# Hybrid encoder block on one core: queue places of seven small products counted over a whole group, and one gate block moved to the second inversion

## The chip, the core and the metric

One core of a Trainium2 chip runs the whole layer. The metric is device time in microseconds (us) of one execution, taken several times; the profile is of one more execution by the hardware profiler. Five engines work side by side, each through its own queue in order: TensorE (PE, matrix products into PSUM banks; its loads of the stationary operand are PEld), VectorE (DVE), ScalarE (ACT), GpSimd (POOL) and SyncE (SP, which here only starts DMA transfers). They wait for each other by semaphores.

## The reference

The input is 2048 tokens of width 1024, in float32, through one layer:

```
h   = RMSNorm(x);  P = h @ w_in          # q/k/v, RWKV-7 r/k/v + low-rank w/a/g, 2048 gate columns
yA  = chunk-band attention               # own chunk of 64 and 8 before it, 8 heads
yB  = RWKV-7 time mixing                 # 8 heads of 64, state 64 x 64, a scan over time
m   = sigmoid(gA) * (yA @ proj_a) + sigmoid(gB) * (yB @ proj_b)
x   = x + RMSNorm(m @ w_out)
x   = x + RMSNorm(relu(RMSNorm(x) @ w_up)^2 @ w_down)
```

The part around the change is yB. A step of its scan is `state = state * w + (state a) b^T + v k^T; y = state r`, and beside each head's output there is a bonus `sum(r * k * r_k) * v`.

## The kernel before

**Precision.** Each large float32 product is made of three: both operands are split into a high part (a cast on ScalarE, L70) and a low part (a subtraction on VectorE, L71), and high x high, high x low and low x high are added in PSUM (`mm3`, L80).

**Dense blocks.** `dense` gives 128 columns of `h @ w_in` for a group of 512 tokens: it loads 512 KB of weights on SyncE's queue (two buffers), splits them, and issues 8 x 3 = 24 products of 128 x 128 by 128 x 512 into one of two banks.

**Groups and stages.** The tokens go in four groups of 512. For each group come `phase_rwkv` (30 dense blocks: 14 of the recurrent branch, 16 gates), `phase_attention` and `phase_merge`; after all groups the feed-forward part follows, in two halves.

**The recurrent stage.** The 8 heads are four pairs (p = 0 to 3; a pair fills 128 partitions), and the scan is made chunk by chunk of 64 tokens:

- `rwkv_pre` projects r, k, v of a pair (three dense blocks, `mix`), forms decays and scaled operands on VectorE, ScalarE and GpSimd, the bonus (L488, two products: high and low part of r), transposes (L497), and the score products inside each chunk (L517): two halves of four chunks, 16 products each, with two banks a half, which VectorE reads into NA, AR and BR (L526 to L533).
- `rwkv_inverse` inverts the chunk matrices of two pairs. VectorE builds the inverses of 32 x 32 blocks by 31 steps, one after the other (L551, L557), then turns them (X1, L560; XD, L562); ScalarE and GpSimd copy XD to XT (L567, L569).
- `rwkv_blocks` completes 64 x 64 from the 32 x 32 blocks: 64 tiny products (L582, NA by X1), a copy to Z on ScalarE (L585), 64 more (L590, Z by XT), a copy to XT (L594).
- `rwkv_trans` makes each chunk's transition out of that (ps_at L609, ps_w L616, ps_ug L626, ps_tq L637, ps_s L650, ps_y L654), and `recurrence` steps through the 8 chunks (L665 to L668). `rwkv_post` normalises (transposes at L693) and writes out.

The first inversion (pairs 0 and 1) has its elimination beside dense blocks of gates and of pair 2, and its transitions between the work of pairs 2 and 3; the second (pairs 2 and 3) stands beside gates alone, near the group's end.

**Order of dense blocks in a group**, counted from 1: low-rank w/a; r, k, v of pair 0; gates 0, 1; r, k, v of pair 1; gates 2, 3; low-rank g; gate 4; r, k, v of pair 2; r, k, v of pair 3; gates 5 to 9; gate 10; gate 11 in the loop over 19 steps of the second transitions at i = 3, gate 12 at i = 9; gates 13, 14, 15 behind it. Each is 24 products, so product 0 of block n has the number 24 (n - 1) in the group's count.

**What sets the order in the queues.** The code is written with generators that are advanced by turns, and a planner then lists each engine's instructions by its own costs and the order written. Where this order isn't wanted, `queue_behind` adds an edge without a semaphore: this product stands behind that one in TensorE's queue. `blocks_behind` uses it for the first product of L582 and of L590: behind products 3 and 12 of the k block of pair 3 (first inversion), and behind products 11 and 20 of gate 11 (second inversion).

Of the kernel before, what the change touches and what calls it, by code (L numbers as in the profile page):

```python
# [32 lines left out]

GATES = (0, 0, 1, 0, 0, 0, 0, 1)
STEPS = (1, 2, 1, 1, 1, 1, 1, 1, 1, 1, 1, 0, 0, 2, 1)
DEC = math.exp(-0.5)

ATT0 = 0
# [12 lines left out]
class Block:  # L51
# [33 lines left out]
        info = mybir.DependencyInfo(mybir.DependencyClass.NoSync, mybir.DependencyReason.DATA)  # L85
        self.tc.add_manual_dep(ins, first.name, info, reason="order of TensorE's queue")

    def blocks_behind(self, *places):

        for ins, i in zip(self.blocks, places):  # L90
            self.queue_behind(ins, self.mm[i])

    def dense(self, col):

        wh, wl = self.wsplit(
            self.a["w_in"][:, col : col + P].rearrange("(k p) n -> p k n", p=P), "w", KB, P
        )
        ps = self.pd.tile([P, G], F32, tag="d", name="psd")
        self.mm = self.mm3(ps, [(wh[:, k], wl[:, k], self.h[0][:, k], self.h[1][:, k]) for k in range(KB)])
        return ps  # L100

    def rstd(self, pool, ssq, scale, eps, post=None):
# [274 lines left out]
    def rwkv_pre(self, g, p, rp, NA, between=lambda: None):  # L377
# [10 lines left out]
        nc.scalar.activation(tw, ps, AF.Tanh, scale=0.5, bias=self.hw0[:, col])  # L388
        k = self.tmp("k")
        self.mix(g, 4 + p, k)  # L390
        if p == 3:
            self.blocks_behind(3, 12)

        ps = self.lora(1, p)
        ta = self.tmp("ta")
# [89 lines left out]

        psb = self.pa.tile([P, G], F32, tag="a", name="ps_bonus")
        for i, x in enumerate((rh, rl)):
            nc.tensor.matmul(psb, self.bones, x, start=i == 0, stop=i == 1)  # L488
        nc.vector.tensor_tensor(r, psb, v, ALU.mult)
        nc.gpsimd.dma_start(self.bvd[p], r)  # L490

# [17 lines left out]
        for h in range(2):  # L509
            cs = slice(h * 4, h * 4 + 4)  # L510

            both = [self.pa.tile([P, 4, P], F32, tag="a", name="ps_A") for _ in range(2)]
            for j in range(4):
                c = h * 4 + j
                for par, psA in enumerate(both):
                    rw = slice(par * C, par * C + C)
                    nc.tensor.matmul(  # L517
                        psA[:, j].rearrange("p (s t) -> p s t", t=C),
                        BK[rw, c].rearrange("p s t -> p (s t)"),
                        AR[rw, c, par : 3 : 2 - par], start=True, stop=True,  # L520
                    )
            for par, psA in enumerate(both):
                ow = slice(C - par * C, P - par * C)
                for lo, w in ((0, C), (32, 32)):
                    hw = slice(par * C + lo, par * C + lo + 32)
                    nc.vector.tensor_tensor(  # L526
                        NA[hw, q, cs, 0:w],
                        psA[hw, :, lo : lo + w],
                        n2[hw, cs, par, None].to_broadcast((32, 4, w)),
                        ALU.mult,  # L530
                    )
                nc.vector.tensor_tensor(AR[ow, cs, par], psA[ow, :, 0:C], mS[ow], ALU.mult)
                nc.vector.tensor_tensor(BR[:, cs, par, 1], psA[:, :, C:P], mN[:, par, cs], ALU.mult)  # L533
# [35 lines left out]
            nc.gpsimd.tensor_copy(XT[par * C : par * C + 32, :, :, 0:32], XD[par * C : par * C + 32])  # L569
        self.X1, self.XT = X1, XT  # L570

    def rwkv_blocks(self, NA, Rs):

        nc, X1, XT = self.nc, self.X1, self.XT
        first, second = [], []
        Z = self.ip.tile([P, 2, NC, 32], F32, tag="Z", name="Z")
        parts = [(slice(r, r + 32), slice(r + 32, r + C)) for r in (0, C)]
        ps = self.pa.tile([P, 2, NC, 32], F32, tag="a", name="ps_t1")
        for q in range(2):
            for c in range(NC):  # L580
                for lo, hi in parts:
                    mm = nc.tensor.matmul(ps[hi, q, c], NA[lo, q, c, 32:64], X1[lo, q, c], start=True, stop=True)  # L582
                    first.append(mm.ins)
        for lo, hi in parts:
            nc.scalar.copy(Z[hi], ps[hi])  # L585
        ps = self.pa.tile([P, 2, NC, 32], F32, tag="a", name="ps_t2")
        for q in range(2):
            for c in range(NC):
                for lo, hi in parts:
                    mm = nc.tensor.matmul(ps[lo, q, c], Z[hi, q, c], XT[hi, q, c, 32:64], start=True, stop=True)  # L590
                    second.append(mm.ins)
        self.blocks = first[0], second[0]
        for lo, hi in parts:
            nc.scalar.copy(XT[lo, :, :, 32:64], ps[lo])  # L594
        for q in range(2):
            Rs[q]["XT"] = XT[:, q]
# [119 lines left out]
    def phase_rwkv(self, g, quads):  # L716
        tc = self.tc
        with ExitStack() as ctx:
            def pool(name, bufs, **kw):
                return ctx.enter_context(tc.tile_pool(name=name, bufs=bufs, reuse_waits="tile", **kw))  # L720

            rp = pool("rw", 3)
            self.tp = pool("rwt", 9)
            self.ip = pool("rwi", 1)
            self.xp = pool("rwx", 2)
            self.lp = pool("rwl", 1)
            self.sp = pool("rws", 2)
            self.pa = pool("rwpa", 2, space=PSUM)
            self.pr = pool("rwpr", 2, space=PSUM)
            self.py = pool("rwpy", 2, space=PSUM)  # L730

            def pairs():
                return self.ip.tile([P, 2, NC, C], F32, tag="NA", name="NA")

            gates = iter(range(2 * KB))

            def gate(n=1):
                for i in range(n):
                    i = next(gates, None)
                    if i is not None:  # L740
                        self.gate(i)

            def places(plan, act):
                it = iter(plan)
                return lambda: act(next(it, 0))

            def rec_of(NA, Rs, b):
                self.rwkv_blocks(NA, Rs)
                yield
                for q in range(2):  # L750
                    yield from self.rwkv_trans(2 * b + q, Rs[q])
                    yield
                yield from self.recurrence(b, Rs)

            self.lora_wa(g)
            NA = pairs()
            between = places(GATES, gate)
            Rs = [self.rwkv_pre(g, q, rp, NA, between) for q in range(2)]
            if g == 0:
                self.bias_corners()  # L760
            inv = self.rwkv_inverse(NA, rp)
            for _ in range(2):
                advance(inv, 8)
                gate()
            advance(inv, 6)
            self.lora_g(g)
            advance(inv)
            gate()
            rec = rec_of(NA, Rs, 0)
            NA = pairs()  # L770
            between = places(STEPS, lambda n: advance(rec, n))
            nxt = [self.rwkv_pre(g, 2 + q, rp, NA, between) for q in range(2)]
            inv = self.rwkv_inverse(NA, rp)
            for n in (1, 4):
                advance(rec, n)
                gate()
            advance(rec)
            post = [self.rwkv_post(q, Rs[q]) for q in range(2)]
            for p in post:
                advance(p, 1)  # L780
            sums = []

            def load(b):
                sums.append(next(quads)(b))
                advance(sums[-1], 1)

            for i in range(3):
                advance(inv, 8)
                gate()
                if i == 0:  # L790
                    b = rp.tile([P, 4, G], F32, tag="BR", name="cmb")
                    load([b[:, i] for i in range(4)])
                elif i == 1:
                    b, c = (rp.tile([P, n, G], F32, tag=t, name="cmb") for t, n in (("AR", 3), ("SV", 2)))
                    load([b[:, 0], b[:, 1], b[:, 2], c[:, 0]])
            advance(inv)
            for p in post:
                advance(p)
            gate()
            rec = rec_of(NA, nxt, 1)  # L800
            load([self.tmp("cmb") for _ in range(4)])
            ops = chain(*sums)
            for i in range(19):
                advance(rec, 1)
                if i == 1:
                    load([self.tmp("cmb") for _ in range(4)])
                if i > 3:
                    advance(ops, 1)
                if i in (3, 9):
                    gate()  # L810
                if i == 3:
                    self.blocks_behind(11, 20)
            advance(rec)
            gate()
            for _ in range(2):
                advance(sums[-1], 2)
                gate()
            post = [self.rwkv_post(2 + q, nxt[q]) for q in range(2)]
            for p in post:
                advance(p, 1)  # L820
            gate(2 * KB)
            for p in post:
                advance(p)

# [680 lines left out]
```

## Time and profile before

| | |
|---|---|
| median of 3 runs | 3324.03 us (3318.0 to 3327.82) |
| profiled execution | 3325.37 us, its span 3323.7 us |
| mean granted TensorE clock | 0.993 |
| TensorE busy | 3198.8 us, 96% of the span |
| VectorE busy | 2248.2 us, 68% |
| ScalarE busy | 1581.6 us, 48% |
| GpSimd busy | 592.7 us, 18% |
| moved by DMA | 592.56 MB |

The span runs from the first to the last instruction; the rest of the profiled execution's time lies around it. A row of a timeline gives start, duration, engine, line, operation, output<-inputs, shapes and count, and in brackets the engine's idle time just before with what ended it. A matrix product's duration covers its way through the array, and the next starts before it ends; the distance between two starts is the rate of issue. Windows give the busy time of each engine in a stretch, the granted TensorE clock (1.00 is full), the DMA share and GB/s. The recurrent stage of the first group lies between 24 and 307 us of the span, those of the other groups end near 791, 1308 and 1828 us.

### The profile page before, as it was taken

To read this page: it belongs to the slowest core of one execution; us is meant where nothing else is said; L and a number is where in the kernel's file an instruction comes from. 1 tells how busy PE (TensorE), PEld (TensorE's weight loads), DVE (VectorE), ACT (ScalarE), POOL (GpSimd) and SP (SyncE) were. 2 spreads that over 40 slices of the span, in tenths; PEclk is the share of its full clock that TensorE was granted. 3 is DMA by queue.
4 is the path that set the end of the run, shared out by engine and by line. 5 is a ranking of instruction groups with operands and counts; after the bars stand their busy time and mean duration, and the time that the engine had idled before them with its cause. 6 is when DMAs were issued, how large, how long until landed. Compare 5 with 4: busy or idle time off the path is not lost. (4 is left out here: it accounts for less than half of the span.)

```text
span 3323.7 us, 50325 instructions
## 1 busy us (share of the span) xinstructions
PE 3198.8 (96%) x18913; PEld 2597.9 (78%) x18913; DVE 2248.2 (68%) x3719; ACT 1581.6 (48%) x2575; POOL 592.7 (18%) x1093
## 2 busy tenths in 40 slices
PE   7999999999999999999999999999999999999998
PEld 5777778777877777877777787878788878788887
DVE  5775666786766876775876675777656757775565
ACT  3434634434644434654444663545543444454333
POOL 2222002222102222101222100121211112220000
PEclk9999999999999999999999999999999999999999
DMA  5335374247465336655325647664787875547565
GB/s 151 89 118 186 114 232 126 80 137 241 156 215 154 91 104 229 198 170 186 96 77 187 208 121 246 231 199 143 240 285 232 300 250 193 168 161 235 191 214 179
DMA packets 449692, 592.56 MB, mean 178 GB/s; under 512 B 26324, under 2 KB 313248, under 8 KB 449448
## 3 DMA queue, kind: packets, MB, share of 16 engines
q1 hardware_dynamic: 392488, 413.14, 40.1%
q0 software_dynamic: 47744, 159.42, 13.2%
q10 hardware_dynamic: 9216, 16.78, 1.4%
q8 instruction: 149, 2.44, 0.3%
q14 instruction: 95, 0.78, 0.1%
HBM read 425.37 MB, written 167.01 MB: 178 GB/s over the span
## 5 line engine op out<-in xcount | busy, mean ns | idle before, releaser
L1341 PE MATMUL ps_dn<-fop 128*128 128x512 f32 x2688 | 613.1, 390 | 2.3 <-DVE fop L71 1.5
L1341 PEld LDWEIGHTS ps_dn<-fop 128*128 128x128 f32 x2688 | 505.3, 188 | 108.2 <-DVE fop L71 2.2
L80 PE MATMUL psd<-hh,whi 128*128 128x512 f32 x1344 | 540.1, 402 | 10.8 <-ACT whi L70 7.6
L80 PE MATMUL psd<-hh,wlo 128*128 128x512 f32 x1344 | 538.1, 400 | 2.7 <-DVE wlo L71 2.6
L80 PE MATMUL psd<-hl,whi 128*128 128x512 f32 x1344 | 539.2, 401 | 0.0
L70 ACT CAST whi<-wraw 128x1024 fp32r<-128x1024 f32 (+1 forms) x296 | 255.5, 864 | 521.6 <-PE psd L80 337.2
L71 DVE TENSOR_TENSOR wlo<-wraw,whi 128x1024 fp32r<-128x1024 f32 (+1 forms) x296 | 292.8, 990 | 223.7 <-ACT whi L70 190.3
L80 PEld LDWEIGHTS psd<-hh,whi 128*128 128x128 f32 x1344 | 255.2, 190 | 61.7 <-ACT whi L70 8.4
L80 PEld LDWEIGHTS psd<-hh,wlo 128*128 128x128 f32 x1344 | 255.0, 190 | 55.1 <-DVE wlo L71 5.2
L80 PEld LDWEIGHTS psd<-hl,whi 128*128 128x128 f32 x1344 | 255.5, 190 | 48.9
L71 DVE TENSOR_TENSOR fop<-xraw,fop 128x1024 fp32r<-128x1024 f32 x112 | 137.1, 1224 | 175.0 <-ACT fop L70 174.3
L70 ACT CAST fop<-xraw 128x1024 fp32r<-128x1024 f32 x112 | 117.7, 1051 | 254.5 <-PE ps_dn L1341 187.5
L1223 POOL DMA_DIRECT2D xd<-X x192 | 103.7, 541 | 392.1 <-ACT X L1220 337.3
L71 DVE TENSOR_TENSOR fop<-wdraw,fop 128x1024 fp32r<-128x1024 f32 x112 | 136.7, 1221 | 23.5 <-ACT fop L70 22.7
L70 ACT CAST fop<-wdraw 128x1024 fp32r<-128x1024 f32 x112 | 117.7, 1051 | 39.8 <-DMA wdraw<-in_w_down_dram 26.1
L903 DVE CUSTOM_DVE_ANT_0 sc<-bias,ps_s 128x640 f32<-128x640 f32 (+4 forms) x128 | 94.0, 734 | 57.0 <-PE ps_pt L914 40.3
L919 DVE TENSOR_TENSOR PTl<-ps_pt,PTh 128x640 fp32r<-128x640 f32 (+4 forms) x128 | 94.4, 738 | 27.7 <-ACT PTh L918 27.2
L70 ACT CAST s12h<-s 128x1024 fp32r<-128x1024 f32 x32 | 33.7, 1052 | 163.7 <-PE ps_u L80 163.7
L908 ACT ACTIVATE sc<-sc,mn 128x640 f32<-128x640 f32 (+4 forms) x128 | 97.6, 762 | 26.1 <-DVE mn L903 25.7
L1066 PE MATMUL ps_o<-whi,mh 128*128 128x512 f32 x256 | 98.8, 400 | 10.2 <-ACT whi L70 8.5
L1066 PE MATMUL ps_o<-wlo,mh 128*128 128x512 f32 x256 | 101.8, 398 | 4.9 <-DVE wlo L71 4.8
L80 PE MATMUL ps_p<-yh,whi 128*128 128x512 f32 x256 | 101.3, 401 | 5.4 <-ACT whi L70 3.6
(368 smaller groups left out, 6823.5 us busy)
## 6 DMA issues: line engine op xcount, KB each, us to landing
wraw<-in_w_in_dram SPq DMA_DIRECT2D x168, 512.0 KB
xraw<-xd SPq DMA_DIRECT2D x112, 512.0 KB
xd<-X POOLq DMA_DIRECT2D x192, 256.0 KB, 5.3
wraw<-in_w_up_dram SPq DMA_DIRECT2D x80, 512.0 KB
wdraw<-wd SPq DMA_DIRECT2D x64, 512.0 KB
wdraw<-in_w_down_dram SPq DMA_DIRECT2D x48, 512.0 KB
gd<-gate ACTq DMA_DIRECT2D x64, 256.0 KB
wd<-cmb POOLq DMA_DIRECT2D x64, 256.0 KB, 3.5
```

Source lines behind the costliest of these rows:

```text
L70: high = self.nc.scalar.copy(hi, src)
L71: self.nc.vector.tensor_tensor(lo, src, hi.bitcast(F32), ALU.subtract)
L80: mm.append(nc.tensor.matmul(ps, l, r, start=n == 0, stop=n == last).ins)
L903: nc.vector.tensor_tensor_reduce(sc[:, 0:n], bias[:, s0:640], pss[:, c0 : c0 + n], 1.0, 3.0e38, ALU.add, ALU.min, mn,)
L908: nc.scalar.activation(sc[:, 0:n], sc[:, 0:n], AF.Exp, scale=-1.0, bias=mn, accum_out=sm[:, col : col + 1])
L919: nc.vector.tensor_tensor(lv, pst[:, 0:nk], hv.bitcast(F32), ALU.subtract)
L1066: nc.tensor.matmul(ps[t], l[:, k, ts], r[:, 0], start=k == 0 and j == 0, stop=k == KB - 1 and j == 2)
L1223: nc.gpsimd.dma_start(self.xd[q][i // 2][:, i % 2], src)
L1341: nc.tensor.matmul(ps, o[:, l, k, sl], o[:, r, k], start=start and n == 0, stop=stop and n == end)
```

## The change

The edges are no longer taken from the block at hand. `dense` keeps all dense products of a group in one list (`dl`, 720 entries), seven small products are noted with a number each, and at the group's end each gets an edge behind the dense product of that number:

| product | before | after |
|---|---|---|
| bonus of pair 0, second product (L488) | no edge | 138 |
| scores of pair 0, first product (L517) | no edge | 150 |
| bonus of pair 1, first product (L488) | no edge | 258 |
| first inversion, first product of L582 | 411 (k of pair 3, product 3) | 412 |
| first inversion, first product of L590 | 420 (k of pair 3, product 12) | 424 |
| second inversion, first product of L582 | 611 (gate 11, product 11) | 623 (gate 11, product 23) |
| second inversion, first product of L590 | 620 (gate 11, product 20) | 632 (gate 12, product 8) |

In the loop over the second transitions two gates (11 and 12) are issued at i = 3 in place of one; gate 13 then comes at i = 9, gates 14 and 15 behind the loop, and one of the calls there finds no gate left. The instructions are the same in number and size.

```diff
+BLOCKS = ((412, 424), (623, 632))
+BONUS = {(0, 1): 138, (1, 0): 258}
+SCORES = 150
...
-    def blocks_behind(self, *places):
-
-        for ins, i in zip(self.blocks, places):
-            self.queue_behind(ins, self.mm[i])
+    def place(self, mm, n):
+
+        self.places.append((mm.ins, n))
+
+    def placed(self):
+
+        for ins, n in self.places:
+            self.queue_behind(ins, self.dl[n])
...
         self.mm = self.mm3(ps, [(wh[:, k], wl[:, k], self.h[0][:, k], self.h[1][:, k]) for k in range(KB)])
+        self.dl += self.mm
...
-        if p == 3:
-            self.blocks_behind(3, 12)
...
-            nc.tensor.matmul(psb, self.bones, x, start=i == 0, stop=i == 1)
+            mm = nc.tensor.matmul(psb, self.bones, x, start=i == 0, stop=i == 1)
+            if (p, i) in BONUS:
+                self.place(mm, BONUS[p, i])
...
+                    if p == c == par == 0:
+                        self.place(mm, SCORES)
...
-        self.blocks = first[0], second[0]
+        for mm, n in zip((first[0], second[0]), BLOCKS[b]):
+            self.place(mm, n)
...
+            self.dl, self.places = [], []
             self.lora_wa(g)
...
-                if i in (3, 9):
+                if i == 3:
+                    gate(2)
+                if i == 9:
                     gate()
-                if i == 3:
-                    self.blocks_behind(11, 20)
...
             gate(2 * KB)
+            self.placed()
```

More of the change, by code (lines that the diff above doesn't have):

```diff
@@ L516, in rwkv_pre @@
                     rw = slice(par * C, par * C + C)
-                    nc.tensor.matmul(
+                    mm = nc.tensor.matmul(
                         psA[:, j].rearrange("p (s t) -> p s t", t=C),
@@ L570, in rwkv_inverse, with rwkv_blocks @@
         self.X1, self.XT = X1, XT
-    def rwkv_blocks(self, NA, Rs):
+    def rwkv_blocks(self, NA, Rs, b):
         nc, X1, XT = self.nc, self.X1, self.XT
@@ L582, in rwkv_blocks @@
                     mm = nc.tensor.matmul(ps[hi, q, c], NA[lo, q, c, 32:64], X1[lo, q, c], start=True, stop=True)
-                    first.append(mm.ins)
+                    first.append(mm)
         for lo, hi in parts:
@@ L590, in rwkv_blocks @@
                     mm = nc.tensor.matmul(ps[lo, q, c], Z[hi, q, c], XT[hi, q, c, 32:64], start=True, stop=True)
-                    second.append(mm.ins)
-        self.blocks = first[0], second[0]
+                    second.append(mm)
+        for mm, n in zip((first[0], second[0]), BLOCKS[b]):
+            self.place(mm, n)
         for lo, hi in parts:
@@ L747, in rec_of @@
             def rec_of(NA, Rs, b):
-                self.rwkv_blocks(NA, Rs)
+                self.rwkv_blocks(NA, Rs, b)
                 yield
```

## The prediction

> **What bounds the kernel now.** I read the page first, then TensorE's list of waits, then the timeline around each product that the diff names, and last the granted clock by windows.
>
> ```profile
> span 3323.7 us, 50325 instructions
> PE 3198.8 (96%) x18913; PEld 2597.9 (78%) x18913; DVE 2248.2 (68%) x3719; ACT 1581.6 (48%) x2575; POOL 592.7 (18%) x1093
> ```
>
> TensorE is busy 96% of the span and no instruction is added or removed, so the time can change only where TensorE stands still, or runs at a lower clock. The list of waits names these at the places of the diff (us in total, times, longest):
>
> ```profile
> PE ps_t L582 <- DVE X L560: 9.6, 4, 2.4
> PE ps_t L590 <- ACT Z L585: 4.4, 9, 0.6
> PE ps_at L609 <- ACT XT L594: 4.0, 4, 1.1
> PE ps_bonus L488 <- ACT rh L70: 4.0, 4, 1.0
> PE ps_A L517 <- DVE BR L533: 2.5, 4, 0.6
> PE ps_bonus L488 <- DVE rl L71: 2.3, 5, 0.5
> ```
>
> There are four groups, so "4 times" is once a group. TensorE works its queue in order: while a small product waits, the dense products behind it stand too, though their operands are there. The whole list here is 27 us, 0.8% of the span. It is the frame for what waits alone can give.
>
> **The second inversion (largest term).** The first product of a block stage, L582, needs X1, the end of VectorE's serial elimination; the second, L590, needs Z, which ScalarE copies out of the first. In the third group:
>
> ```profile
> 1250.40 0.39 PE L80 MATMUL psd<-hh,wlo 128*128 128x512 f32 x1
> 1253.17 1.20 PE L582 MATMUL ps_t<-X,NA 32*32 32x32 f32 x64 [2.38 <-DVE X L560]
> 1254.64 0.39 PE L80 MATMUL psd<-hl,whi 128*128 128x512 f32 x1
> 1254.87 0.39 PE L80 MATMUL psd<-hh,wlo 128*128 128x512 f32 x1
> 1256.75 0.24 PE L590 MATMUL ps_t<-XT,Z 32*32 32x32 f32 x2
> 1258.47 0.66 PE L609 MATMUL ps_at<-ident,AR 128*128 128x128 f32 x4
> ```
>
> Dense products issue every 0.23 us (1254.64 to 1254.87). The old places are the 12th and 21st product of the gate block issued at i = 3; that block is the 26th dense block of its group, so in the group's count they are 611 and 620. The new ones are 623 and 632: 12 products more before each, 12 x 0.23 = 2.7 us of work against a wait of 2.4 us. These 12 come out of the gates' end of the group, so they are no extra work. The wait at L582 should go to nothing, with only 0.3 us to spare.
>
> At L590 the start is set by Z, that is by VectorE and ScalarE, and 12 more products will stand before it: the most that the two moves can give is 2.7 us a group. What can take some back is ScalarE. The last group:
>
> ```profile
> 1769.70 1.07 DVE L560 STREAM_TRANSPOSE X<-X 128x512 f32<-128x512 f32 x1
> 1770.66 1.18 DVE L71 TENSOR_TENSOR wlo<-wraw,whi 128x1024 fp32r<-128x1024 f32 x1
> 1771.76 0.70 DVE L562 STREAM_TRANSPOSE XD<-X 128x512 f32<-128x512 f32 x1
> 1772.49 1.25 ACT L567 COPY XT<-XD 32x512 f32<-32x512 f32 x2 [5.37 <-DVE XD L562]
> 1773.77 1.18 ACT L585 COPY Z<-ps_t 32x512 f32<-32x512 f32 x2
> 1782.18 1.05 ACT L70 CAST whi<-wraw 128x1024 fp32r<-128x1024 f32 x1
> 1783.27 1.22 DVE L71 TENSOR_TENSOR wlo<-wraw,whi 128x1024 fp32r<-128x1024 f32 x1 [7.83 <-ACT whi L70]
> ```
>
> The cast at 1782.18 needs the weight buffer of the block that the change finishes before L582, so it and that gate's tanh become ready near 1771 and can stand ahead of the copies. If both fit into ScalarE's room before 1772.49, Z is 0.3 to 0.4 us late; if they stand between XT and Z, 1.7 us. I take 0.3, since the room is there: 2.7 - 0.3 = 2.4 us a group, **9.6 us**; bounds 4 (1.7 late) and 10.9 (nothing late).
>
> The gate that moves from i = 9 to i = 3 takes its weight load on SyncE's queue and its store on ScalarE's along. Between those two points SyncE's queue has only gate loads, and the combinations' transfers go by POOL's, so it passes nobody. Each later gate moves up one place and the last stretch loses one block; its cover falls by 12 products at the places of the diff, and the closing transposes have no wait today:
>
> ```profile
> L693 PE MATMUL ps_yt<-ident,yn 128*64 128x128 f32 x128 | 18.5, 272 | 0.0
> ```
>
> I cost that at nothing. Without that cover the 12 products' 2.7 us would come back as waiting.
>
> **The clock behind that wait.** The same place in the last and first group, and the granted clock over ten us in all four:
>
> ```profile
> 251.51 1.61 PE L582 MATMUL ps_t<-X,NA 32*32 32x32 f32 x64 [2.40 <-DVE X L560]
> 257.53 0.65 PE L609 MATMUL ps_at<-ident,AR 128*128 128x128 f32 x4
> 1770.82 1.87 PE L582 MATMUL ps_t<-X,NA 32*32 32x32 f32 x64 [2.43 <-DVE X L560]
> 1773.22 0.63 PE L80 MATMUL psd<-hl,whi 128*128 128x512 f32 x1
> 1773.64 0.63 PE L80 MATMUL psd<-hh,wlo 128*128 128x512 f32 x1
> 1778.28 0.66 PE L609 MATMUL ps_at<-ident,AR 128*128 128x128 f32 x4
> 251.00:261.00 10.00, 9.43 (x182) 0.83 0.60 160
> 735.30:745.30 10.00, 9.37 (x182) 0.83 0.52 159
> 1252.60:1262.60 10.00, 8.89 (x185) 1.00 0.58 171
> 1770.30:1780.30 10.00, 9.48 (x149) 0.66 0.58 164
> ```
>
> After the wait the clock (third figure from the end of a window's row) was cut in three groups of four, and dense products issue every 0.42 us in place of 0.23. From L582 to the transposes took 5.3 us in the third group at full clock, 6.0 in the first, 7.5 in the last: 0.7 and 2.2 us lost, and 0.7 for the second group with the first's clock: **3.6 us** that should go with the wait. Bounds: nothing, and 0.17 + 0.17 + 0.34 of 10 us, 6.8.
>
> [...]
>
> **Bonus and scores of the first pair.** In the last group:
>
> ```profile
> 1588.68 0.50 PE L488 MATMUL ps_bonus<-rl,bones 128*128 128x512 f32 x1 [0.53 <-DVE rl L71]
> 1595.56 1.13 PE L517 MATMUL ps_A<-AR,BK 64*128 64x128 f32 x8 [0.64 <-DVE BR L533]
> 1625.14 0.50 PE L488 MATMUL ps_bonus<-rh,bones 128*128 128x512 f32 x1 [1.00 <-ACT rh L70]
> ```
>
> Counting dense rows from the group's start, 135 stand before the first of these; the new place makes it 139, 0.9 us for a wait of 0.53: **2.1 us** over four groups (bounds 0 and 2.8, with some 0.15 us of restart each). The scores' first product goes from 144 to 151, 1.6 us later; its second half, which waits for the first half's banks, stands 8 products behind it and I expect it to be listed with the same distance. VectorE's reads of the first half stand behind a weight split (1.2 us by the rows above) today, so they slip by less than the 1.6; 0.64 of it must be left over, and I take it that it is: **2.5 us**, bounds 0 (the second half is not moved) and 2.8. VectorE is fed by TensorE after both, so what is gained is kept.
>
> **Second pair's bonus and first inversion: capped.** The bonus goes from 253 to 259 (1.4 us against 1.0), the block products from 412 to 413 and from 421 to 425. Counted singly they would give 4.0 for the bonus and 3 or more for L590. But from that bonus on VectorE is full:
>
> ```profile
> 1636.00:1669.00 33.00, 33.00 (x165) 27.05 (x165) 31.29 (x81) 14.27 (x21) 4.62 (x10) 1.00 0.32 92
> 1666.98 1.16 DVE L560 STREAM_TRANSPOSE X<-X 128x512 f32<-128x512 f32 x1
> 1668.67 1.20 PE L582 MATMUL ps_t<-X,NA 32*32 32x32 f32 x64
> 1672.78 0.24 PE L590 MATMUL ps_t<-XT,Z 32*32 32x32 f32 x2 [0.64 <-ACT Z L585]
> 1685.52 0.42 DVE L640 TENSOR_TENSOR TQ<-ps_tq,id 128x256 f32<-128x256 f32 x1 [8.42 <-PE ps_tq L637]
> ```
>
> Over 33 us VectorE (third busy figure) works 31.3, so X1 does not come sooner because TensorE arrives sooner. TensorE now reaches L582 0.5 us after X1 (1668.14 to 1668.67); 6 - 1 = 5 products, 1.1 us, sooner it stands there for some 0.6 us, a new wait. What is behind it in TensorE's queue waits with it, and L590 still stands for Z. So to L590's start, which the VectorE chain fixes, the gain is what its place allows: 4 products more, 0.9 us a group, **3.7 us**. After it VectorE waits for TensorE (8.42 us), so this is kept. L609's wait for XT (1.1) stays. Bounds: 0 if the chain itself comes 0.9 us later; 8 if it comes sooner and the waits of L488 and L590 really go.
>
> **Sum.** 9.6 + 3.6 + 2.1 + 2.5 + 3.7 = 21.5 us. The profiled execution took 3325.4 us (span 3323.7 and 1.7 around it), 1.3 above the median 3324.0 of its runs. 3325.4 - 21.5 = 3303.9, less 1.3: **3303 us**, 0.6% faster. A measurement of this kernel tells 0.3%, 10 us, from no change: under 3314 counts as faster.
>
> **Rivals.**
>
> 1. Only the second inversion gains. All queues are listed anew, and the four small moves (8.3 us) are given back as waits a few products on, the first inversion's L582 first. For: VectorE's 31.3 of 33 us. Against: its 8.42 us idle just after, and its waits for TensorE around the first pair. 3303 + 8 = 3311.
> 2. The cut clock has another cause than the wait, say the long run of small products, and stays; the 3.6 us do not come: 3306. For: the third group waited as long, at full clock. Against: the cut begins at L582 each time. [...]
> 3. The first inversion's chain moves up too, and its waits go: 8 in place of 3.7 us, and ScalarE has room in the second inversion (10.9): 3303 - 4.3 - 1.3 = 3297. Against: the same 31.3 of 33.
> 4. Slower. The second L590 now stands behind 9 products of the next gate, the second of which needs that gate's low weights. Today the split lies at 1770.66, between X1 and XD. If the new listing puts it where the next split stands (ends 1784.5), TensorE stands at that dense product, and L590 behind it starts at 1784.5 + 8 x 0.23 = 1786.3, where 1770.82 + 3.6 = 1774.4 is expected: 11.9 us late, less 2.7, 9.2 a group, 37 in all, and a cut clock stays. 3324 + 37 - 8 = 3353. From 4.8 us late on (2.7 and 2.1 of the other moves), a split that ends after 1777.4, the change costs time. Against: the row shows that split listed right behind X1 while its gate stood later in the program; the change only brings it forward.
> 5. The places do not bind. Against: all seven are above today's counts, so each must move; nothing then is left but noise: 3324.
>
> **How the numbers follow.** Forecast 0.55, rivals 0.14, 0.09, 0.10, 0.07 and 0.05. Of rival 1, so near 3314, two thirds count as faster; so 0.55 + 0.09 + 0.09 + 0.10 = 0.83, less the forecast's own tail where several terms sit at their lower bounds at once: 0.81 faster, 0.12 same, 0.07 slower. The range takes in rivals 1 to 3 and the bounds of the two largest terms: from 3303 - 1.3 - 3.2 - 4.3 - 2 (restarts) = 3292 to 3303 + 5.6 + 3.6 + 6 (the second inversion and the clock at their lower bounds, and 6 of the 8.3 us of the small moves gone) = 3318. The forecast's own range is 3297 to 3309.
>
> **What will show it.** In the list of waits, L582 falls from 9.6 to about 2.5 us, all of it new and in the first inversions; L488 from 6.3 to under 1.5; L517 from 2.5 to under 0.5; L609's 4.0 stays, L590 keeps 3 to 5. The granted clock of ten us around each second inversion is 1.00 in at least three groups. A wait of "PE psd L80" for wlo behind the second L582, or L582 still at 2 us there, would make the prediction wrong.

## The result, and the profile after

| | before | changed |
|---|---|---|
| median, measured beside each other | 3329.48 us (20 runs) | 3319.49 us (20 runs) |
| changed / before | | 0.9971, 95% interval 0.9963 to 0.9979 |
| profiled execution, its span | 3325.37, 3323.7 us | 3319.16, 3317.3 us |

The change saves 9.6 us by the ratio (0.29%), where 21.5 were forecast. It is faster, but by just under the 0.3% that the prediction called its bound. The median of the kernel before is 5 us higher over 20 runs than over its first three, so the ratio is what is compared with the forecast: 3303/3324 would be 0.9937. One of the eight executions of e11 below took 3907 us, at a granted clock of 0.75; its median includes that one, its ratio doesn't.

Lines of the changed kernel are shifted: L494, L505, L525, L592, L600, L620, L676, L697, L704 and L83 are L488, L497, L517, L582, L590, L609, L665, L686, L693 and L80 of before. (The experiments' lines differ by a few: in e1, e3 and e11 the first and second product of a block stage are L590 and L598.) The counts of PE, PEld, DVE, ACT and POOL are those of before; the 7 instructions less are of the kinds that don't count as busy. Its page and TensorE's list of waits (us in total, times, longest):

```profile
span 3317.3 us, 50318 instructions
PE 3200.5 (96%) x18913; PEld 2593.2 (78%) x18913; DVE 2246.3 (68%) x3719; ACT 1582.7 (48%) x2575; POOL 595.4 (18%) x1093
...
PE psd L83 <- ACT gate L724: 6.8, 8, 1.2
PE ps_at L620 <- ACT XT L605: 4.4, 4, 1.1
PE ps_st L676 <- DVE ST L679: 2.8, 4, 0.7
PE ps_bk L505 <- DVE BR L509: 2.7, 4, 0.7
PE ps_g L83 <- DVE yn L697: 2.3, 4, 0.6
PE ps_t L600 <- ACT Z L595: 2.2, 8, 0.4
PE ps_bonus L494 <- DVE rl L74: 2.0, 4, 0.5
```

The waits that were aimed at have gone: L592 for X (9.6) is down to 0.8, L525 for BR (2.5) is no longer listed, L600 for Z fell from 4.4 to 2.2, the bonus from 6.3 to 2.0. Of the signs that the prediction named, those for L517, L609 and the clock came; the bonus stayed above its 1.5, and L592 and L600 fell further than its 2.5 and 3 to 5. But three rows are new: a dense product that waits for a gate's tanh to read its bank (6.8, twice a group), the transposes L505 (2.7, once), and the closing products L83 of ps_g (2.3, once).

**Reading by stretches.** All kernels have the same 720 dense products in a group. So the distance between the starts of two of them, by their number, can be compared between traces, whatever small products lie between. The first and the 720th of the third group, before and changed:

```profile
1037.64 0.39 PE L80 MATMUL psd<-hh,whi 128*128 128x512 f32 x1
...
1304.92 0.39 PE L80 MATMUL psd<-hh,wlo 128*128 128x512 f32 x1
```
```profile
1032.92 0.39 PE L83 MATMUL psd<-hh,whi 128*128 128x512 f32 x1
...
1297.08 0.39 PE L83 MATMUL psd<-hh,wlo 128*128 128x512 f32 x1
```

267.28 us became 264.16. In pieces, in us (third group, where both traces show a granted clock of 1.00 over the whole stretch):

| products | what lies there | before | changed | |
|---|---|---|---|---|
| 120 to 168 | bonus and scores of pair 0 | 18.51 | 17.86 | -0.65 |
| 240 to 288 | bonus of pair 1 | 18.45 | 18.31 | -0.14 |
| 408 to 456 | first inversion, its transitions | 45.06 | 44.48 | -0.58 |
| 456 to 504 | first recurrence, pair 3 | 25.10 | 26.47 | +1.37 |
| 504 to 600 | gates 7 to 10 | 25.75 | 24.95 | -0.80 |
| 600 to 719 | second inversion and recurrence | 57.01 | 54.69 | -2.32 |

The other pieces agree within 0.02. The 3.1 us a group are 12.5 us over four; 9.6 are left in the time. The next rows show what was won where, and what was lost behind the stretch.

**The second inversion.** The changed kernel at the place shown of before, and the windows of 10 us behind L592 in all four groups (the granted clock is the third figure from the end):

```profile
1247.93 1.20 PE L592 MATMUL ps_t<-X,NA 32*32 32x32 f32 x64
...
1252.35 1.19 PE L600 MATMUL ps_t<-XT,Z 32*32 32x32 f32 x62 [0.20 <-ACT Z L595]
```
```profile
251.30:261.30 10.00, 9.21 (x188) 7.27 (x189) 4.84 (x6) 7.75 (x14) 4.88 (x7) 1.00 0.74 231
731.90:741.90 10.00, 9.23 (x188) 7.28 (x189) 4.85 (x6) 7.75 (x14) 4.88 (x7) 1.00 0.74 226
1247.90:1257.90 10.00, 9.23 (x188) 7.28 (x189) 4.85 (x6) 7.75 (x14) 4.89 (x7) 1.00 0.76 219
1765.00:1775.00 10.00, 9.23 (x188) 7.30 (x189) 4.83 (x6) 7.74 (x14) 4.87 (x7) 1.00 0.76 239
```

No wait at L592, 0.20 us at L600, and a clock of 1.00 where it was 0.83, 0.83, 1.00 and 0.66.

**The first recurrence.** The same group of the changed kernel, TensorE, ScalarE and VectorE around dense product 482:

```profile
1201.03 0.39 PE L83 MATMUL psd<-hl,whi 128*128 128x512 f32 x1
1202.59 0.50 PE L83 MATMUL psd<-hh,whi 128*128 128x512 f32 x1 [1.17 <-ACT gate L724]
1202.92 0.40 PE L83 MATMUL psd<-hl,whi 128*128 128x512 f32 x1
1204.02 0.33 PE L676 MATMUL ps_st<-ST,TQ 64*64 64x64 f32 x4 [0.70 <-DVE ST L679]
...
1200.77 1.05 ACT L73 CAST whi<-wraw 128x1024 fp32r<-128x1024 f32 x1 [1.18 <-PE psd L83]
1201.85 0.69 ACT L724 ACTIVATE gate<-psd,hgb 128x512 f32<-128x512 f32 x1
...
1202.23 1.44 DVE L473 SCALAR_TENSOR_TENSOR r<-r,cst,tk 128x512 f32<-128x512 f32 x1
1203.60 0.46 DVE L679 SCALAR_TENSOR_TENSOR ST<-ps_st,gC,S 128x64 f32<-128x64 f32 x2
1203.99 1.21 DVE L74 TENSOR_TENSOR wlo<-wraw,whi 128x1024 fp32r<-128x1024 f32 x1
```

And the wait of before at this place:

```profile
1210.54 0.33 PE L665 MATMUL ps_st<-ST,TQ 64*64 64x64 f32 x4 [0.97 <-DVE ST L668]
```

Two products of gate 6 are done at 1201.03; its third needs the low weights that VectorE makes at 1203.99, behind pair 3's operands and the state ST. So the new listing puts the first two products of gate 7 here. They need the bank of gate 5, which ScalarE reads only at 1201.85, behind a cast. Then L676 waits for ST. Before, it was this one wait of 0.97 us for ST, at dense product 490; now there are 1.17 + 0.70 = 1.87 us, at 484, so six products (1.4 us) that had filled the wait still lie ahead. The other four of the eight waits for a gate's tanh are 0.52 us each, right behind L592 of the second inversion.

**The closing products.** The third group's end, changed, with the first dense product behind it, and that product before:

```profile
1297.31 1.03 PE L704 MATMUL ps_yt<-ident,yn 128*64 128x128 f32 x8
...
1298.79 0.69 DVE L697 TENSOR_TENSOR yn<-ps_y,grs 128x512 f32<-128x512 f32 x1 [2.07 <-POOL grs L695]
...
1299.63 0.70 PE L83 MATMUL ps_g<-lora_g,g2h 128*128 128x512 f32 x2 [0.59 <-DVE yn L697]
...
1300.40 0.39 PE L83 MATMUL psd<-hh,whi 128*128 128x512 f32 x1
```
```profile
1307.40 0.39 PE L80 MATMUL psd<-hh,whi 128*128 128x512 f32 x1
```

The last product of the second recurrence stands behind 685 dense products of the group, before behind 661, so 35 are left to cover what follows it where there were 59; and yn, through VectorE, GpSimd and VectorE again, is late. From the 720th dense product of the group to the next dense product it took 2.48 us before (1304.92 to 1307.40) and takes 3.32 now (1297.08 to 1300.40). That is 0.84 us a group, 3.4 in all, outside the stretch.

### The profile page after: what moved, and what is told of

Read it like the earlier page. It is cut to its first block, busy times and chain, and to the rows that moved or that the text cites. A ratio compares the mean times of both kernels' runs of the same rounds, so it can differ in the third digit from the quotient of the medians.

```text
span 3317.3 us, 50318 instructions
## 1 busy us (share of the span) xinstructions
PE 3200.5 (96%) x18913; PEld 2593.2 (78%) x18913; DVE 2246.3 (68%) x3719; ACT 1582.7 (48%) x2575; POOL 595.4 (18%) x1093
## 5 line engine op out<-in xcount | busy, mean ns | idle before, releaser
L83 PE MATMUL psd<-hh,whi 128*128 128x512 f32 x1344 | 541.1, 403 | 16.9 <-ACT whi L73 7.0
L83 PE MATMUL psd<-hh,wlo 128*128 128x512 f32 x1344 | 536.2, 399 | 1.1 <-DVE wlo L74 1.1
L83 PE MATMUL psd<-hl,whi 128*128 128x512 f32 x1344 | 536.2, 399 | 0.0
L83 PEld LDWEIGHTS psd<-hh,whi 128*128 128x128 f32 x1344 | 254.2, 189 | 70.6 <-ACT whi L73 9.6
L83 PEld LDWEIGHTS psd<-hh,wlo 128*128 128x128 f32 x1344 | 254.0, 189 | 53.0 <-DVE wlo L74 2.6
L83 PEld LDWEIGHTS psd<-hl,whi 128*128 128x128 f32 x1344 | 254.3, 189 | 47.7
L932 DVE TENSOR_TENSOR PTl<-ps_pt,PTh 128x640 fp32r<-128x640 f32 (+4 forms) x128 | 94.4, 738 | 26.5 <-ACT PTh L931 25.9
L83 PE MATMUL ps_p<-yh,whi 128*128 128x512 f32 x256 | 101.4, 402 | 6.1 <-ACT whi L73 5.5
```

The lines of the kernel that those rows point to most:

```text
L83: mm.append(nc.tensor.matmul(ps, l, r, start=n == 0, stop=n == last).ins)
L932: nc.vector.tensor_tensor(lv, pst[:, 0:nk], hv.bitcast(F32), ALU.subtract)
```

## The experiments

All diffs are against the changed kernel. "Stretch" is the third group's time from dense product 0 to 719, or the shortest of groups 2 to 4 where the third has a cut of the clock (in e11 all have one). Times are medians.

| | time | before beside it | ratio, 95% interval | stretch |
|---|---|---|---|---|
| changed | 3319.49 | 3329.48 | 0.9971, 0.9963 to 0.9979 | 264.1 |
| e1 second inversion alone | 3319.73 | 3326.79 | 0.9986, 0.9977 to 0.9995 | 265.7 |
| e2 all but it | 3319.14 | 3326.79 | 0.9981, 0.9970 to 0.9992 | 266.2 |
| e3 as e1, old gates | 3319.41 | 3326.79 | 0.9980, 0.9970 to 0.9989 | 265.9 |
| e4 no bonus edges | 3310.98 | 3326.79 | 0.9960, 0.9947 to 0.9972 | 263.8 |
| e5 changed again | 3316.19 | 3326.49 | 0.9971, 0.9959 to 0.9982 | 264.2 |
| e6 blocks in turn | 3321.63 | 3326.49 | 0.9986, 0.9974 to 0.9998 | 264.7 |
| e7 scores and second | 3318.03 | 3326.49 | 0.9979, 0.9968 to 0.9989 | 264.9 |
| e8 as e4, old gates | 3315.46 | 3326.49 | 0.9966, 0.9954 to 0.9979 | 264.2 |
| e9 as e4, again | 3317.33 | 3327.84 | 0.9970, 0.9956 to 0.9983 | 263.8 |
| e10 as e4, no gate at i = 9 | 3318.07 | 3327.84 | 0.9965, 0.9953 to 0.9978 | 264.1 |
| e11 second inversion earlier | 3336.63 | 3327.84 | 1.0021, 1.0006 to 1.0036 | 269.8 |
| e12 as e4, split before r | 3312.85 | 3327.84 | 0.9954, 0.9941 to 0.9966 | 263.3 |
| e13 as e12 and e10 | 3310.06 | 3328.50 | 0.9950, 0.9938 to 0.9963 | 263.7 |
| e14 three gates at i = 3 | 3345.89 | 3328.50 | 1.0057, 1.0045 to 1.0070 | 263.8 |
| e15 changed, third time | 3317.87 | 3328.50 | 0.9972, 0.9962 to 0.9982 | 264.2 |

**e1, e2, e3: the second inversion alone, the small moves alone.**

```diff
# e1 and e3
-BLOCKS = ((412, 424), (623, 632))
-BONUS = {(0, 1): 138, (1, 0): 258}
+BLOCKS = ((411, 420), (623, 632))
+BONUS = {}
...
-                    if p == c == par == 0:
-                        self.place(mm, SCORES)
# e2
-BLOCKS = ((412, 424), (623, 632))
+BLOCKS = ((412, 424), (611, 620))
# e2 and e3
-                if i == 3:
-                    gate(2)
-                if i == 9:
+                if i in (3, 9):
                     gate()
```

> Only the second inversion's two places (623, 632) and the moved gate; the first inversion at its old places (411, 420), no edge for bonus and scores. If the second inversion is the whole of the change's gain and the clock does not count in the median: 2.3 us a group less in the recurrent stage, 0.75 of it given back at the closing products, 6 us in all. If the clock behind the old wait counts as in the profile before (3.6 us): 10 us. If the small moves carry the gain: under 3 us.

> Bonus, scores and the first inversion's places as after; the second inversion and the gates as before. As the prediction had it (2.1 + 2.5 + 3.7): 8 us less. If these are given back as new waits a few products on, above all a dense product that waits 1.2 us for its bank behind a gate: -0.6 us a group, 2.5 us in all, and that wait is in this run's list four times.

> As the run with the second inversion's places alone, but the gates stay at i = 3 and i = 9. If the moved gate makes the closing products late (0.6 us at ps_g, four times), this wait is gone and the time is 3 us less than with the moved gate. If the places make it late, the wait stays. If the moved gate is needed so that the 12 products come in time, the second inversion waits again, 2 us a group.

Products 600 to 720 take 57.0 us before and 55.4 in e1: 1.65 us a group, 6.6 in four, not the 9.3 of the whole change. The wait for X is gone in e1 too; what is left is one for Z, 1.4 us a group here (9.5 us listed for both inversions). ScalarE in e1, and in the changed kernel:

```profile
1251.18 1.25 ACT L575 COPY XT<-XD 32x512 f32<-32x512 f32 x2 [5.44 <-DVE XD L570]
1252.45 1.05 ACT L73 CAST whi<-wraw 128x1024 fp32r<-128x1024 f32 x1
1253.52 1.18 ACT L593 COPY Z<-ps_t 32x512 f32<-32x512 f32 x2
```
```profile
1247.63 1.24 ACT L577 COPY XT<-XD 32x512 f32<-32x512 f32 x2 [4.21 <-DVE XD L572]
...
1250.04 1.05 ACT L73 CAST whi<-wraw 128x1024 fp32r<-128x1024 f32 x1 [0.45 <-ACT gate L724]
1251.12 1.18 ACT L595 COPY Z<-ps_t 32x512 f32<-32x512 f32 x2
```

In both the cast stands between XT and Z, as the prediction feared. In e1 XT starts 1.5 us after the block products (1249.66 in its trace), so Z is late; in the changed kernel it starts 0.3 us ahead of them, since there the elimination is done earlier: X ends 213.9 us behind the group's first dense product, in e1 215.7. e3 has the old gates and no wait for yn, so that wait came with the gates; its time is that of e1 within the error. In e2 the stretch falls by 1.05 us: the small moves are worth about 4 us, and the two parts (1.65 + 1.05 = 2.7) come near the whole (3.1). The wait of 1.17 us for the bank is in e2's list four times, as its second expectation had it. By the ratios e1, e2 and e3 save 4.7, 6.3 and 6.7 us, each with an error of 3 to 4, so the times alone can't tell these parts.

**e4, e9: without the bonus edges.**

```diff
-BONUS = {(0, 1): 138, (1, 0): 258}
+BONUS = {}
```

> The changed kernel without the two edges of the bonus. If the bonus moves give nothing (the first only hands its wait on to the next transposes, the second is given back by the full VectorE): same time as the changed kernel within 2 us, 9 to 11 us under before. If they gave what was predicted (2.1 and up to 4): 3 to 6 us slower than the changed kernel. If the new wait at the bank comes from them: 5 us faster.

> The changed kernel without the two bonus edges once more, as the base of the runs beside it. Theory (the bonus edges only move waits of the VectorE chain on, and cost 0.37 us a group by the third group's stretch, 263.8 against 264.2 us): 1 to 5 us below the changed kernel, ratio to the kernel before 0.996. Rival (its first time, 3311, was low by chance): 0.997.

The stretch is 0.37 us shorter than with them. Products 120 to 168 take 17.83 us with and without the edge of pair 0: its wait for rl (0.53) only became the wait of L505 for BR (0.68). The edge of pair 1 saves 0.17 us on the spot and costs 0.57 at the first inversion (44.48 against 43.9), where X1 comes 0.8 us later. So both are worth nothing or less. The wait of 1.17 us for the bank is in e4's list as well, so it doesn't come from these edges. e4's ratio, 3.7 us better than the changed kernel's, did not come again: e9 has 0.9970. A cost of 1.5 us (4 x 0.37) can't be seen in these runs.

**e5, e6: the early products of gate 7.**

```diff
# e6: the first product of gate 7 behind the last of gate 6
+            self.places.append((self.dl[504], 503))
             self.placed()
```

> The changed kernel once more, so that the next three stand beside it on one chip. Both theories: about 0.3% faster than before (ratio 0.997), and the third group's stretch from its first to its 720th dense product takes 264.2 us, as in its first profile.

> The changed kernel with one edge more a group: the 505th dense product (the first of gate 7) stands behind the 504th, so the early start of two products of gate 7, with its wait of 1.17 us for the bank, is gone. Theory (the new listing's bank wait costs what it shows): the third group's stretch falls from 264.2 to 263.0 us, the whole by 4 to 5 us against the changed kernel. Rival (the two products were put ahead because the low weights of gate 6 come late, and TensorE waits for those instead): 264.0 or more, the whole within 1 us of the changed kernel.

e5 repeats the ratio (0.9971) and the stretch of the changed kernel. For e6 the theory falls. The wait for the bank is gone in e6, but this row takes its place:

```profile
PE ps_st L676 <- DVE ST L679: 10.4, 4, 2.6
```

2.6 us a group against 1.17 + 0.70, the stretch 0.5 us longer, the whole 5.4 us slower than e5 on the same chip; the stretch explains 2 of these, and the ratios (0.9986 and 0.9971) have errors of 4 us each. The two early products filled a wait that comes anyway; VectorE's ST and the split behind it are late, not the bank.

**e7: without the first inversion's moves.**

```diff
-BLOCKS = ((412, 424), (623, 632))
-BONUS = {(0, 1): 138, (1, 0): 258}
+BLOCKS = ((411, 420), (623, 632))
+BONUS = {}
```

> The changed kernel without the two bonus edges and with the first inversion at its old places (411, 420); the scores, the second inversion and the gate stay. Theory (the first inversion's later places bring the early start of gate 7, but also save 0.6 us of waiting there and keep Z of the second inversion in time): no bank wait of 1.17 us, the wait for Z in the second inversion back at 1.2 to 1.4 us, the third group's stretch 264.4 us (the kernel without the two bonus edges alone: 263.8), the whole 2 to 3 us above that one. Rival (the first inversion's places cost more than they give): 263.2 us and 2 us below it.

No early products, and Z late again (9.3 us listed for L600), both as the theory has it; the stretch is 264.9, half a us above its figure. Against e4 products 408 to 456 cost 1.14 us more, 456 to 504 save 1.40, 504 to 600 cost 0.75, and the late Z 0.6. So the first inversion's move does save its 1.1 us, and gives back more (1.4) at the recurrence behind it; it gets that back at gates 7 to 10 and at the second inversion.

**e12: is it VectorE's order there?** Pair 3's product r (1.44 us above) is put behind gate 6's split.

```diff
 # e4, and in rwkv_pre, split and dense:
-        nc.vector.scalar_tensor_tensor(r, r, self.rk[:, col], tk, op0=ALU.mult, op1=ALU.mult)
+        rr = nc.vector.scalar_tensor_tensor(r, r, self.rk[:, col], tk, op0=ALU.mult, op1=ALU.mult)
+        if p == 3:
+            self.late.append(rr.ins)
...
-        self.nc.vector.tensor_tensor(lo, src, hi.bitcast(F32), ALU.subtract)
+        low = self.nc.vector.tensor_tensor(lo, src, hi.bitcast(F32), ALU.subtract)
+        self.low = low.ins
...
+        self.lows.append(self.low)
...
-            self.dl, self.places = [], []
+            self.dl, self.places, self.lows, self.late = [], [], [], []
...
             self.placed()
+            self.queue_behind(self.late[0], self.lows[20])
```

> As the kernel without the bonus edges, with one edge on VectorE's queue: pair 3's product r x r_k x k (1.44 us) stands behind the weight split of gate 6. Theory (at the 483rd dense product TensorE does not lack a bank but VectorE: step 5 of the first recurrence and gate 6's split stand behind pair 3's operands on it): the state ST and the split come 1.4 us sooner, the waits of 1.17 and 0.70 us there fall to about 0.5 together, the third group's stretch from 263.8 to 262.4 to 262.8 us, 4 to 5 us in all. Rival (VectorE is full, so pair 3's bonus, come later, stops TensorE instead): 263.6 or more, with a wait at pair 3's bonus or transposes.

The order in e12, and the state ST in e9, which lacks only this edge:

```profile
1203.01 0.48 DVE L683 SCALAR_TENSOR_TENSOR ST<-ps_st,gC,S 128x64 f32<-128x64 f32 x2
1203.40 1.58 DVE L74 TENSOR_TENSOR wlo<-wraw,whi 128x1024 fp32r<-128x1024 f32 x1
1204.91 0.74 DVE L475 SCALAR_TENSOR_TENSOR r<-r,cst,tk 128x512 f32<-128x512 f32 x1
```
```profile
1203.36 0.46 DVE L679 SCALAR_TENSOR_TENSOR ST<-ps_st,gC,S 128x64 f32<-128x64 f32 x2
```

The third group starts at 1034.01 in e12's trace and at 1033.09 in e9's, so ST comes at 169.0 in place of 170.3 us of the group, 1.3 us sooner where the theory had 1.4. No wait for the bank is left; that for ST is 1.25 us a group (5.0 in all), and some 0.25 for wlo: 1.5 us together where the theory had 0.5 and e9 has 1.87. The stretch falls by 0.5 us, half or less of what the theory had and more than the rival. The time is 4.5 us below e9 on the same chip (5 and 6 runs), of which the stretch explains 2. So VectorE's order does set these waits, but it explains only part of them: with the bank's wait gone TensorE is at this step sooner too, and waits again.

**e8, e10, e14: the closing products.**

```diff
# e8: e4 and
-                if i == 3:
-                    gate(2)
-                if i == 9:
+                if i in (3, 9):
                     gate()
# e10: e4 and
-                if i == 9:
-                    gate()
# e14: e4 and
                 if i == 3:
-                    gate(2)
+                    gate(3)
```

> The changed kernel without the two bonus edges, and with gates 11 and 12 at i = 3 and i = 9 again, one each; the places stay. Theory (the closing transposes lost their cover with the gate that moved): the wait of TensorE for yn at the closing products (2.3 us in four) goes, 0.75 us a group, 3 us in all: 3308 where the kernel without the bonus edges took 3311; Z of the second inversion stays as it was there. Rival (the 0.75 us only moves on to the next stage, or the second inversion pays for it as gate 12's weights come later): 3311 to 3314.

> As the kernel without the bonus edges, but the call for a gate at i = 9 is left out: gates 11 and 12 at i = 3, and 13, 14, 15 behind the loop, so the second recurrence stands 24 dense products earlier in TensorE's queue. Theory (the closing transposes wait because only one gate's work is left behind the recurrence): the waits for yn at the closing products (2.3 us in four) go, 0.75 us a group, 3 us in all, with the third group's stretch at 263.8 us as without the bonus edges. Rival (the recurrence, come earlier, takes the time back with waits for ST inside the loop): stretch 264.2 or more, no gain.

> As the kernel without the bonus edges, but three gates are called at i = 3 and one at i = 9, so the second recurrence ends 24 dense products later: 11 of them, 2.5 us, are left behind it as cover for the closing transposes, where 35 (8 us) were. Theory (the closing wait is real time, set by the chain recurrence, yn, transposes): TensorE waits some 5.4 us more a group at the closing products (24 x 0.23), 22 us in all: 3335 to 3342. Rival (what the profile shows there is made up elsewhere, since the gates stand earlier and take waits away in the loop): under 3325.

e8 and e10 list no wait for yn, and their stretch is 0.37 us longer (for e10 as the rival had it), so 0.4 to 0.5 us a group should be left. Neither time shows it. e14 shows that the wait is real time:

```profile
PE ps_s L910 <- DMA KK<-kc: 9.8, 3, 3.9
...
PE ps_yt L704 <- DVE yn L697: 6.2, 4, 1.5
PE ps_g L83 <- DVE yn L697: 6.0, 4, 1.5
```

With 24 products less of cover 12.2 us of waits for yn are listed in place of 2.4, and attention then waits 9.8 us for a transfer that it did not wait for before. The whole is 28 us slower than e15 on the same chip, with the stretch as in e9; more than the 22 expected, and 8 more than these waits add up to (19.6), which stay unexplained. Over all kernels but e14, take the time's difference to before, less four times the difference of the stretch to 267.28: the nine with the wait for yn have +1.7 us on the mean, the six without it (e2, e3, e8, e10, e11, e13) -1.0. The 2.7 us between them (error about 1.3) agree with the 3.4 of the rows.

**e11: a longer wait at the second inversion.**

```diff
 # e1's edits but BLOCKS, the old gates, and
+BLOCKS = ((411, 420), (599, 608))
```

The places 599 and 608 don't bind: the planner's own order puts these products behind 606 and 615 dense products.

> The kernel before in all but the second inversion, which has no binding place: its first products stand behind dense products 606 and 615 in place of 612 and 621, so TensorE waits longer for X1, by 6 x 0.23 = 1.4 us: 3.8 in place of 2.4 us. Theory (the wait cuts the clock behind it): each of the four groups shows a half-clock window of 3.4 or 6.8 us at the second inversion; the wait costs 5 to 6 us over four groups and the clock another 3 or more beyond before's: 3333 to 3337. Rival (the cut belongs to the run of small products): clock as before, at most 3332, and windows in two or three groups as now.

```profile
PE ps_t L590 <- DVE X L568: 15.0, 4, 3.8
...
251.90:261.90 10.00, 9.89 (x183) 7.94 (x184) 4.51 (x6) 5.08 (x11) 4.22 (x7) 0.83 0.62 180
736.90:746.90 10.00, 10.00 (x150) 7.59 (x150) 4.53 (x6) 4.17 (x8) 4.22 (x7) 0.66 0.62 181
1258.90:1268.90 10.00, 9.88 (x183) 7.95 (x184) 4.53 (x6) 5.08 (x11) 4.22 (x7) 0.83 0.59 177
1777.10:1787.10 10.00, 9.88 (x183) 7.82 (x183) 4.53 (x6) 5.02 (x10) 4.22 (x7) 0.83 0.57 167
```

The wait is 3.75 us a group and the clock is cut behind it in four groups of four, in place of three: with no wait none of four, as shown above. The half-clock windows of the expectation are those of before's trace: a granted clock of 0.50 from 252.0 to 255.4 us in the first group and from 1771.0 to 1777.8 in the last. The run of small products is the same in all three kernels, so the cut belongs to the wait. All traces together say the same of this place: with a wait of 1.4 us or more for X or Z (before, e1, e2, e3, e7, e11) the clock is cut in 16 of 24 groups, in the other eleven traces in none of 44. By the ratio e11 takes 7.0 us more than before, 5.4 of them the wait itself.

**e13, e15: the better version.** e13 has e12's edge and e10's gates.

> Both edits together: pair 3's product behind the split of gate 6, and no gate called at i = 9. Theory (the two waits are at different places and add): the third group's stretch 0.5 us under the same without the first edit (263.6 against 264.1 us), no wait for yn; 1 to 3 us under the kernel with the split alone. Rival (what the gates give at the closing products they take in the loop): equal to the kernel with the split alone, 3313, within 1.5 us.

> The changed kernel a third time, as the base of the two runs beside it. Both theories: ratio 0.997 to the kernel before; the kernel with both edits (split and gates) 4 to 7 us below it.

e13 beats both kernels: 0.9950 of before, and 7.8 us under the changed kernel on the same chip. Against e12 it gains 1.3 us by the ratios, where the rows give 1.9 (0.84 less 0.37 of a longer stretch, four times); the errors are larger than either, so that the parts add is not shown by the times.

## Why the prediction was right and wrong

In us over four groups, by the prediction's own terms:

| term | predicted | measured |
|---|---|---|
| second inversion | 9.6 | 9.3 |
| clock behind its wait | 3.6 | 3.8 gone there, some 2 lost elsewhere |
| bonus of pair 0 | 2.1 | 0 |
| scores of pair 0 | 2.5 | 2.6 to 2.7 |
| bonus of pair 1 and first inversion | 3.7 | 2.9, then 2.3 given back |
| closing cover | 0 | -3.4 |
| sum | 21.5 | 11 by these rows, 9.6 (7.0 to 12.3) by the times |

- **Second inversion: the wait and the size right, one step wrong.** The wait at L582 went, as the sum had it. But the prediction took it that cast and tanh would fit in ahead of XT; the cast stands between XT and Z, the case that it had priced at its lower bound. In e1 that price shows (TensorE waits 1.4 us a group for Z, and the step is worth 6.6 us in all). In the changed kernel XT comes early through the other moves, and nothing is lost. The sum had no term for that, so 9.3 against 9.6 is in part luck.
- **Scores: right.** They are the one small move whose saving stayed whole (e7 against e1: 18.51 to 17.84 us a group).
- **Bonus of pair 0: failed.** The step counted 4 products against a wait of 0.53 and asked only whether the bonus would still wait. It did not ask what stands next: the transposes L505 need BR from the same VectorE, which had not come sooner.
- **Pair 1 and first inversion: the cap was right, the last sentence wrong.** "After it VectorE waits for TensorE (8.42 us), so this is kept." That gap was one of its place (and 8.42 is of the one group whose clock was cut there, to a mean of 0.54 from 1675 to 1680 us; in the third group it is 6.45). Some 35 us behind it, pair 3's operands and the recurrence fill VectorE again (5.0 us busy in the five before the wait at dense product 484), and products moved ahead of one wait are missing at the next. Of the 2.9 us, 5.5 were given back there and 3.2 regained behind (the wait for low weights at gate 8 went). This is the first rival's mechanism, some 60 products on rather than a few.
- **Closing cover: failed.** The prediction saw that the last stretch loses a block, but counted 12 products less of cover, where the traces show 24 (59 to 35), and took a list without waits as room enough. The list shows that TensorE did not wait, not by how much it did not. It wrote itself that without cover the 2.7 us "would come back as waiting"; 0.84 a group did.
- **Clock: right in its place, wrong in the sum.** The cut left the second inversion, where it had cost 3.8 us in the one trace of before, and e11 confirms that it hung on the wait. But cuts came behind the new waits (last section): 4 in the 12 groups of the three traces of the changed kernel, 1.2 us each, so 1.6 us an execution. The times can't settle what is left: 9.6 less the other terms gives 0.4 us, with an error of 2.7, and the part of the execution outside the stretches and closings takes from 2223 to 2236 us in the traces but e14's.

The slower rival (a split that comes late behind L600) did not show: no wait for wlo stands there.

## What to carry to other kernels

When an in-order queue is filled up ahead of a wait, ask where those instructions came from: the wait at that later place, and the slack of places that show no wait, belong into the sum. Before counting a wait as gain, follow the engine that ends it to the next thing that it must deliver; at the bonus of pair 0 that was BR, from the same VectorE, and the wait of 0.53 us for rl became one of 0.68. Fix the order on the late engine (e12: one edge on VectorE, 4.5 us) rather than that of the waiting one (e6: one edge on TensorE, 5.4 us lost).

## What the runs showed of the hardware

The clock was cut behind shorter waits than the 2.4 us that the prediction saw, down to 1.0 us in two parts (3 groups of 20, below). In products 456 to 504, nine traces have the wait of 1.17 us for the bank and, 1.4 us behind it, that of 0.70 us for ST (changed, e2, e4, e5, e8, e9, e10, e14, e15): in 15 of their 36 groups the stretch takes 27.7 us in place of 26.5, with a cut of the granted clock in it (0.83 over ten us in the second row below). In the 20 groups of the five traces with one wait of 0.97 us there (before, e1, e3, e7, e11) there is none, and the stretch is 25.1 each time. Two groups of e5, without and with the cut, in the 10 us behind that wait:

```profile
687.20:697.20 10.00, 9.24 (x102) 6.75 (x102) 9.61 (x21) 1.22 (x2) 3.26 (x6) 1.00 0.62 189
1205.30:1215.30 10.00, 9.30 (x98) 7.19 (x98) 8.46 (x18) 1.07 (x2) 3.21 (x6) 0.83 0.51 145
```

Over the nine traces that is 0.5 us a group, 2 us an execution: about half of what the second inversion's cuts had cost. In all traces, a cut followed

| wait | groups with a cut behind it |
|---|---|
| 3.75 us for X (e11) | 4 of 4 |
| 2.6 us for ST (e6) | 3 of 4 |
| 2.4 us for X (before) | 3 of 4 |
| 1.53 us for X (e2) | 2 of 4 |
| 1.4 us for Z, in two parts (e1, e3, e7) | 7 of 12 |
| 1.25 us for ST (e12, e13) | 3 of 8 |
| 1.17 us for the bank, then 0.70 for ST | 15 of 36 |
| 1.0 us for Z at the first inversion, in two parts (before, e1, e3, e7, e11) | 3 of 20 |
| 1.0 us for rh, at the bonus of pair 1 (twelve traces) | 0 of 48 |
| 0.97 us for ST (before, e1, e3, e7, e11) | 0 of 20 |

In these traces the share of groups with a cut falls from 4 of 4 behind 3.75 us to 3 of 88 behind 1.0 us and less, though not row by row (1.25 us: 3 of 8, 1.17 and 0.70: 15 of 36). Whether the length alone decides is open: the places differ in what stands around the wait, and only at the second inversion (before, e11) did a run change the length and little else.
